# Softmax over rows of 512 on one core: two late tiles of 15 and 13 rows in place of four, and the first load issued by SyncE

## Chip, cores, metric

One core of a Trainium2 chip. The metric is the device time of one execution in microseconds (us), median of several executions. The span is the time from the first to the last instruction of the program in the profile; it is 1.8 us shorter than the device time.

## The reference

The input is 16 x 1024 x 512 in float32, 33.55 MB; so is the output.

```python
def reference(x):                       # x: (16, 1024, 512) float32
    x_scaled = x / 2.0
    x_max = np.max(x_scaled, axis=-1, keepdims=True)
    exp_x = np.exp(x_scaled - x_max)
    return (exp_x / np.sum(exp_x, axis=-1, keepdims=True)).astype(np.float32)
```

## The kernel before

The 16,384 rows are laid over 128 partitions, so each partition has 128 rows of 2 KB; "row" from here on means one such row in all partitions (262,144 B). A buffer of 100 rows in SBUF holds the tiles. PLAN lists them: the chunks of rows that are computed together, and the place in the buffer. The first eight tiles (100 rows) are loaded at once; the tiles t8 to t11 reuse the place of stored ones and must wait for those stores.

```python
PLAN = [
    ([3], 0), ([4, 3], 3), ([5] * 3, 10), ([5] * 3, 25), ([5] * 3, 40), ([5] * 3, 55),
    ([5] * 3, 70), ([5] * 3, 85), ([5] * 3, 10), ([4, 3], 3), ([3], 0), ([3], 25),
]
ARENA = 100
LAG = 2
AFTER = {8: 4, 9: 4, 10: 4, 11: 6}    # late load t8 is issued after the exps of tile 4, ...
FUSED = {1, 2, 3}
...
def issue_loads(begin, end):           # tiles 0 and 1 ahead of the start-up barrier
    for t in range(begin, end):
        if t not in behind:            # behind: tiles that reuse another's place
            nc.scalar.dma_start(out=sb(t), in_=dram(xf, t)).then_inc(ld[t], 16)
...
        # ACT (ScalarE): late loads between the exps; exp with the sum accumulated
        for k, (t, b, c, a) in enumerate(chunks):
            while late and last_chunk[AFTER[late[0]]] < k:
                u = late.pop(0)
                for v in behind[u]:
                    nc.scalar.wait_ge(st[v], 16)
                nc.scalar.dma_start(out=sb(u), in_=dram(xf, u)).then_inc(ld[u], 16)
            ...                        # c exps, the first waits for the chunk's max
        # DVE (VectorE): max of chunk k, then reciprocal and multiply of chunk k - 2
        for k in range(len(chunks) + LAG):
            if k < len(chunks):
                do_max(k)              # waits for the tile's load
            if k >= LAG:
                do_mul(k - LAG)        # waits for the chunk's exps
        # SP (SyncE): a tile is stored when its last chunk is multiplied
        for t in range(len(tiles)):
            nc.sync.wait_ge(s_mul, last_chunk[t] + 1)
            nc.sync.dma_start(out=dram(of, t), in_=sb(t)).then_inc(
                st[t] if t in awaited else s_end, 16
            )
        # GpSimd closes the program
        for t in awaited:
            nc.gpsimd.wait_ge(st[t], 16)
        nc.gpsimd.wait_ge(s_end, 16 * (len(tiles) - len(awaited)))
```

Of the kernel before, what the change touches and what calls it, by code (L numbers as in the profile page):

```python
# [1 line left out]

# [4 lines left out]




PLAN = [
    ([3], 0), ([4, 3], 3), ([5] * 3, 10), ([5] * 3, 25), ([5] * 3, 40), ([5] * 3, 55),
    ([5] * 3, 70), ([5] * 3, 85), ([5] * 3, 10), ([4, 3], 3), ([3], 0), ([3], 25),
]
ARENA = 100
LAG = 2

AFTER = {8: 4, 9: 4, 10: 4, 11: 6}

FUSED = {1, 2, 3}  # L20


@with_exitstack
def kernel(
    ctx: ExitStack,
    tc: tile.TileContext,
    x: bass.AP,
    out: bass.AP,
):
    nc = tc.nc  # L30
    fp32 = mybir.dt.float32

    xf = x.flatten_outer_dims()
    of = out.flatten_outer_dims()
    N, D = xf.shape
    P = nc.NUM_PARTITIONS
    n_rows = N // P
    assert sum(sum(c) for c, _ in PLAN) == n_rows

    arena = nc.alloc_sbuf_tensor("arena", (P, ARENA, D), fp32)  # L40
    negmax = nc.alloc_sbuf_tensor("negmax", (P, n_rows), fp32)
    sums = nc.alloc_sbuf_tensor("sums", (P, n_rows), fp32)
    recip = nc.alloc_sbuf_tensor("recip", (P, n_rows), fp32)



    tiles, chunks, base = [], [], 0
    for t, (cs, at) in enumerate(PLAN):
        r = sum(cs)
        tiles.append((base, r, at))  # L50
        o = 0
        for c in cs:
            chunks.append((t, base + o, c, at + o))
            o += c
        base += r
    last_chunk = {c[0]: k for k, c in enumerate(chunks)}

    def dram(ap, t):
        b, r, _ = tiles[t]
        return ap[b * P : (b + r) * P].rearrange("(p r) d -> p r d", r=r)  # L60

    def sb(t):
        _, r, at = tiles[t]
        return arena[:, at : at + r, :]


    behind = {}
    for t, (_, r, at) in enumerate(tiles):
        for u in range(t):
            _, ru, au = tiles[u]  # L70
            if at < au + ru and au < at + r:
                behind.setdefault(t, []).append(u)

    ld = [tc.alloc_semaphore(f"ld{t}") for t in range(len(tiles))]
    awaited = sorted({u for us in behind.values() for u in us})
    st = {t: tc.alloc_semaphore(f"st{t}") for t in awaited}
    s_end = tc.alloc_semaphore("s_end")
    s_max = tc.alloc_semaphore("s_max")
    s_exp = tc.alloc_semaphore("s_exp")
    s_rec = tc.alloc_semaphore("s_rec")  # L80
    s_mul = tc.alloc_semaphore("s_mul")

    def issue_loads(begin, end):

        for t in range(begin, end):
            if t not in behind:
                nc.scalar.dma_start(out=sb(t), in_=dram(xf, t)).then_inc(ld[t], 16)

    def do_max(k):
        t, b, c, a = chunks[k]  # L90
        nc.vector.reduce_max(  # L91
            out=negmax[:, b : b + c],
            in_=arena[:, a : a + c],
            axis=mybir.AxisListType.X,
            negate=True,
        )._wait_ge(ld[t], 16).then_inc(s_max, 1)

    def do_mul(k):
        t, b, c, a = chunks[k]
        nc.vector.reciprocal(  # L100
            out=recip[:, b : b + c], in_=sums[:, b : b + c]
        )._wait_ge(s_exp, k + 1).then_inc(s_rec, 1)
        if t in FUSED:
            nc.vector.tensor_mul(  # L104
                out=arena[:, a : a + c],
                in0=arena[:, a : a + c],
                in1=recip[:, b : b + c].unsqueeze(2).to_broadcast([P, c, D]),
            )._wait_ge(s_rec, k + 1).then_inc(s_mul, 1)
            return
        for r in range(c):  # L110
            ins = nc.vector.tensor_scalar_mul(  # L111
                out=arena[:, a + r],
                in0=arena[:, a + r],
                scalar1=recip[:, b + r : b + r + 1],
            )
            if r == 0:
                ins._wait_ge(s_rec, k + 1)
        ins.then_inc(s_mul, 1)

    def compute_and_store():  # L120

        late = sorted(behind)
# [6 lines that stand above are left out]
            for r in range(c):  # L129
                ins = nc.scalar.activation(  # L130
                    out=arena[:, a + r],
                    in_=arena[:, a + r],
                    func=mybir.ActivationFunctionType.Exp,
                    bias=negmax[:, b + r : b + r + 1],
                    scale=0.5,
                    accum_out=sums[:, b + r : b + r + 1],
                )
                if r == 0:
                    ins._wait_ge(s_max, k + 1)
            ins.then_inc(s_exp, 1)  # L140


        for k in range(len(chunks) + LAG):
            if k < len(chunks):
                do_max(k)
            if k >= LAG:
                do_mul(k - LAG)
# [5 lines that stand above are left out]
                st[t] if t in awaited else s_end, 16  # L153
            )

        for t in awaited:
            nc.gpsimd.wait_ge(st[t], 16)
        nc.gpsimd.wait_ge(s_end, 16 * (len(tiles) - len(awaited)))



    hook = nc.inst_callbacks[-1]
    nc.remove_inst_callback(hook)
    symbolic = nc._always_lower_symbolic_ap
    nc._always_lower_symbolic_ap = False
    here = str(nc.cur_bb)
    entry = nc.main_func.blocks[0]
    head, jumps = entry.instructions[:-5], entry.instructions[-5:]
    entry.instructions = []
    nc.switch_bb("main", None)  # L170
    issue_loads(0, 2)
    first = list(entry.instructions)
    at = next(k for k, i in enumerate(head) if type(i).__name__ == "InstDrain")
    entry.instructions = head[:at] + first + head[at:]
    issue_loads(2, len(tiles))
    compute_and_store()
    entry.instructions = list(entry.instructions) + jumps
    nc.switch_bb(here, None)
    nc._always_lower_symbolic_ap = symbolic
    nc.push_inst_callback(hook)  # L180


# [1 line left out]
_INS = ['x']  # L184
_OUTS = [((16, 1024, 512), 'float32')]


# [23 lines left out]
```

## Time and profile before

| | before |
|---|---|
| device time | 162.19 us (162.18 to 162.22, 4 runs) |
| span | 160.4 us |
| first DMA packet starts, last one ends | 1.14 us, 158.94 us |
| DVE's last multiply ends | 152.6 us |
| last store issued | 152.62 us |

Three kinds of numbers are used. The page gives busy shares over the span and over 40 equal slices. The table of stretches gives, for each stretch of time, each engine's busy time and what the DMA engines moved in it. The trace also has one record for every DMA packet (start, duration, size, queue); packet times and the ends of the 16 DMA engines are worked out from these records. They do not name the engine, so "the slowest engine" is the last packet to end, and "the mean engine" comes from joining packets end to start into 16 chains. The lines themselves stand in the prediction.

### The profile page before, as it was taken

To read this page: it belongs to the slowest core of one execution; us is meant where nothing else is said; L and a number is where in the kernel's file an instruction comes from. 1 tells how busy PE (TensorE), PEld (TensorE's weight loads), DVE (VectorE), ACT (ScalarE), POOL (GpSimd) and SP (SyncE) were. 2 spreads that over 40 slices of the span, in tenths; PEclk is the share of its full clock that TensorE was granted. 3 is DMA by queue.
4 is the path that set the end of the run, shared out by engine and by line. 5 is a ranking of instruction groups with operands and counts; after the bars stand their busy time and mean duration, and the time that the engine had idled before them with its cause. 6 is when DMAs were issued, how large, how long until landed. Compare 5 with 4: busy or idle time off the path is not lost.

```text
span 160.4 us, 480 instructions
## 1 busy us (share of the span) xinstructions
DVE 132.0 (82%) x155; ACT 94.5 (59%) x257; POOL 0.2 (0%) x4
## 2 busy tenths in 40 slices
DVE  0475499999999999999999999999999997704900
ACT  0739076759548646866679666697666875500500
POOL 0000000000000000000000000000000000000000
DMA  7999999999998999999999999998999999999796
GB/s 259 483 402 467 397 426 411 343 464 420 417 483 383 475 391 467 429 429 439 414 460 406 467 391 469 398 467 376 474 432 423 441 429 432 411 448 432 335 408 245
DMA packets 3459, 67.13 MB, mean 419 GB/s; under 512 B 384, under 2 KB 384, under 8 KB 1152
## 3 DMA queue, kind: packets, MB, share of 16 engines
q10 hardware_dynamic: 1728, 33.56, 49.5%
q1 hardware_dynamic: 1728, 33.56, 48.8%
q14 instruction: 3, 0.02, 0.0%
HBM read 33.55 MB, written 33.55 MB: 418 GB/s over the span
## 4 chain that ended last, share of the span: by engine, by line
DVE 49%; DMA 38%; another core or an unknown queue 5%; ACT 1%; issue 0%; DVEq 0%
DMA arena<-in_x_dram 38%; DVE negmax L91 25%; DVE arena L104 13%; DVE arena L111 10%; ACT arena L130 1%; DVE recip L100 1%; DVEq L206 0%
## 5 line engine op out<-in xcount | busy, mean ns | idle before, releaser
L130 ACT ACTIVATE arena<-arena,negmax 128x512 f32<-128x512 f32 x128 | 90.8, 710 | 51.6 <-DVE negmax L91 51.6
L91 DVE TENSOR_REDUCE negmax<-arena 128x5 f32<-128x2560 f32 (+2 forms) x28 | 72.3, 2586 | 19.6 <-DMA arena<-in_x_dram 19.5
L111 DVE TENSOR_SCALAR arena<-arena,recip 128x512 f32<-128x512 f32 x91 | 37.9, 482 | 0.7
L130 ACT ACTIVATION_READ_ACCUMULATOR arena<-arena,negmax 128x1 f32 x128 | 23.9, 187 | 0.0
L104 DVE TENSOR_TENSOR arena<-arena,recip 128x2560 f32<-128x2560 f32 (+2 forms) x8 | 21.0, 2625 | 0.3
L100 DVE RECIPROCAL recip<-sums 128x5 f32<-128x5 f32 (+2 forms) x28 | 4.9, 176 | 0.0
L130 ACT ACT_TABLE_LOAD x1 | 1.3, 1283 | 4.5 <-issue 4.5
L195 POOL MEMSET const-bfloat16-1.0<- 128x1 bf16 x1 | 0.1, 101 | 0.0
L195 POOL MEMSET const-uint8-127<- 128x1 uint8 x1 | 0.1, 101 | 0.0
L195 POOL MEMSET const-float32-0.0<- 128x1 f32 x1 | 0.1, 98 | 0.2 <-issue 0.2
L195 POOL MEMSET const-float32-1.0<- 128x1 f32 x1 | 0.1, 98 | 0.0
## 6 DMA issues: line engine op xcount, KB each, us to landing
arena<-in_x_dram ACTq DMA_DIRECT2D x7, 3840.0 KB, 44.9
out_dram<-arena SPq DMA_DIRECT2D x7, 3840.0 KB, 23.1
arena<-in_x_dram ACTq DMA_DIRECT2D x2, 1792.0 KB, 33.1
out_dram<-arena SPq DMA_DIRECT2D x2, 1792.0 KB, 11.7
arena<-in_x_dram ACTq DMA_DIRECT2D x3, 768.0 KB, 52.2
out_dram<-arena SPq DMA_DIRECT2D x3, 768.0 KB, 6.7
```

Source lines behind the costliest of these rows:

```text
L91: nc.vector.reduce_max(out=negmax[:, b : b + c], in_=arena[:, a : a + c], axis=mybir.AxisListType.X, negate=True,)._wait_ge(ld[t], 16).the ...
L100: nc.vector.reciprocal(out=recip[:, b : b + c], in_=sums[:, b : b + c])._wait_ge(s_exp, k + 1).then_inc(s_rec, 1)
L104: nc.vector.tensor_mul(out=arena[:, a : a + c], in0=arena[:, a : a + c], in1=recip[:, b : b + c].unsqueeze(2).to_broadcast([P, c, D]),)._w ...
L111: ins = nc.vector.tensor_scalar_mul(out=arena[:, a + r], in0=arena[:, a + r], scalar1=recip[:, b + r : b + r + 1],)
L130: ins = nc.scalar.activation(out=arena[:, a + r], in_=arena[:, a + r], func=mybir.ActivationFunctionType.Exp, bias=negmax[:, b + r : b + r ...
L195: nc = _bacc.Bacc("TRN2", target_bir_lowering=False, num_devices=1)
```

## The change

The four late tiles of 15, 7, 3 and 3 rows become two of 15 and 13 rows, placed at the start of the buffer. The first load goes from ACT to SyncE, so that the first two loads are issued by two engines at the same time. GpSimd's four waits for stores that the late loads already depend on are dropped. The intent is fewer, larger transfers and an earlier start. A line that differs in whitespace alone is cut.

```diff
-    ([5] * 3, 70), ([5] * 3, 85), ([5] * 3, 10), ([4, 3], 3), ([3], 0), ([3], 25),
+    ([5] * 3, 70), ([5] * 3, 85), ([5] * 3, 0), ([5, 4, 4], 15),
 ]
...
-AFTER = {8: 4, 9: 4, 10: 4, 11: 6}
+AFTER = {8: 4, 9: 6}
...
         for t in range(begin, end):
-            if t not in behind:
+            if t in behind:
+                continue
+            if t == 0:
+                nc.sync.dma_start(out=sb(t), in_=dram(xf, t)).then_inc(ld[t], 16)
+            else:
                 nc.scalar.dma_start(out=sb(t), in_=dram(xf, t)).then_inc(ld[t], 16)
...
-        for t in awaited:
-            nc.gpsimd.wait_ge(st[t], 16)
         nc.gpsimd.wait_ge(s_end, 16 * (len(tiles) - len(awaited)))
```

## The prediction

> **What bounds the kernel now.** I read the page first, parts 1 to 3, to see which resource is full for the whole span.
>
> ```profile
> span 160.4 us, 480 instructions
> DVE 132.0 (82%) x155; ACT 94.5 (59%) x257; POOL 0.2 (0%) x4
> DVE  0475499999999999999999999999999997704900
> DMA  7999999999998999999999999998999999999796
> q10 hardware_dynamic: 1728, 33.56, 49.5%
> q1 hardware_dynamic: 1728, 33.56, 48.8%
> ```
>
> The reader is to see two nearly full rows. DVE is solid from slice 6 to slice 32, but has idle slices at both ends. The DMA row has no hole: the load queue (q10) and the store queue (q1) together take 98.3% of what 16 engines can give in the span. So bytes bound this kernel, and DVE is a close second that must only not starve the stores.
>
> Second, the table of stretches (us, DVE busy, ACT busy, POOL busy, clock, DMA share, GB/s) for the end, where this change acts.
>
> ```profile
> 130.00:140.00 10.00, 8.07 (x15) 5.94 (x17) 0.00 (x0) 1.00 0.98 420
> 140.00:145.00 5.00, 0.00 (x0) 0.00 (x0) 0.00 (x0) 1.00 1.06 452
> 145.00:150.00 5.00, 3.28 (x7) 1.57 (x5) 0.00 (x0) 1.00 0.94 406
> 150.00:152.00 2.00, 1.97 (x6) 0.66 (x2) 0.00 (x0) 1.00 0.82 344
> 152.00:154.00 2.00, 0.59 (x2) 0.00 (x0) 0.00 (x0) 1.00 1.01 423
> ```
>
> DVE does nothing from 140 to 145, and still the DMA engines are full. The only weak place is 150 to 152. (A share takes a packet whole at its start, so it can exceed 1; clipping the packet records at the edges of the stretch, I find 0.75 there, 0.98 for 148 to 150 and 1.00 or more in every stretch of 2 us from 2 to 148.) The bubble is 2 x 0.25 + 2 x 0.02 = 0.54 us of mean engine time, all there is to win by better feeding.
>
> Third, the timeline of DVE, for why the last loads are late.
>
> ```profile
> 126.24 2.28 DVE L91 TENSOR_REDUCE negmax<-arena 128x4 f32<-128x2048 f32 x1
> 135.70 1.75 DVE L91 TENSOR_REDUCE negmax<-arena 128x3 f32<-128x1536 f32 x1 [1.11 <-DMA arena<-in_x_dram]
> 146.65 1.75 DVE L91 TENSOR_REDUCE negmax<-arena 128x3 f32<-128x1536 f32 x1 [7.40 <-DMA arena<-in_x_dram]
> 151.32 1.28 DVE L111 TENSOR_SCALAR arena<-arena,recip 128x512 f32<-128x512 f32 x3
> ```
>
> The last load, 768 KB, lands at 146.6, 11.0 us after the one before it, although 0.79 MB alone would take under 2 us. The traffic of the stretch 126 to 142 shows why (packets, MB, share of 16 engines):
>
> ```profile
> q1 hardware_dynamic: 218, 5.71, 82.8%
> q10 hardware_dynamic: 220, 1.25, 18.7%
> ```
>
> Equal packets, very unequal bytes: each DMA engine takes one load packet, then one store packet. A packet here is one partition's rows. The trace's DMA records give its time: 234 ns for 6,144 B (3 rows), 535 ns for 14,336 B (7 rows), 1,138 ns for 30,720 B (15 rows). A tile puts 8 packets on each engine, so 3 rows against a 15-row store need 8 x (234 + 1138) = 11.0 us, as seen.
>
> **What the Trainium skill says.** The page "DMA: Bandwidth & Descriptors", section "Queues, rings and completion order", says that an engine goes round-robin over the queues with work, a packet at a time. The trace agrees (218 against 220 packets). Its section "Issuing engines are not separate DMA queues" says that issuing from several engines saves only the sequencer's issue time; this trace has ACT at 376 ns for the first issue, and no run here yet shows SyncE issuing a load. Its section "Where 436 GB/s comes from" has a ceiling of 435.2 GB/s for the 16 ports. Taking that figure, 67.11 MB need an estimated 154.2 us; the first packet starts at 1.14 us and the last ends at 158.93, so 157.8 us are used, and only some 3.6 us could go even with perfect packets. The page "Perfetto Trace Analysis", section "What “DMA-bound” means", counts engines that are full as a bound and says larger descriptors are what matters then; the change does go that way, but from packets that are already 6 KB and more.
>
> **The change part by part.** The tiles t0 to t8 keep their sizes, 3, 7 and seven of 15 rows. The last 13 rows were three tiles (7, 3, 3) and become one (13, in chunks of 5, 4, 4).
>
> (a) Packets. Per queue and engine the three tiles took 8 x (535 + 234 + 234) = 8.02 us. A 13-row packet has 26,624 B; between the 7- and 15-row packets the time grows by 603 ns per 16,384 B, so I estimate 1138 - 0.151 x 1000 = 987 ns, and 8 x 987 = 7.90 us. Saved: 0.13 us per queue, 0.25 us for both; four semaphore writes of 9 ns less make 0.29 us. This lies on the bounding resource and counts in full.
>
> (b) The order of loads and stores. The 13-row load gets almost half the engine against 15-row stores: 8 x (987 + 1138) = 17.0 us. The load before it ends at 109.92 in the records, so its packets end at 126.9 and, with the 1.5 us from last packet to landing that t8 and t11 show, it lands near 128.4 instead of having its last part at 146.6. That only moves bytes: stores done in that time are fewer by as much.
>
> (c) Does DVE still feed the stores? A step of 5 rows takes 2.73 (max) + 0.1 + 2.07 (multiply) = 4.93 us. Maxes of t8 start at 111.45, 116.4, 121.3; the multiply of t8's first chunk ends at 126.3. DVE then waits to 128.4 for the 13 rows, does max of 5 (to 131.2), multiply (133.4), max of 4 at 2.28 (135.6), multiply (137.8): t8's store goes out near 137.8, against 134.6 before. Then max of 4 (139.9), multiply 5 (142.1), multiplies of 4 at 1.8 (143.9, 145.7): the last store goes out near 145.8, against 152.6. The store queue meanwhile: t7's store, pushed back by the larger load packets, ends near 141.0 to 141.6; t8's 9.1 us end at 150.1 to 150.7; the last 7.9 us end near 158.4. Each store is queued 3 us or more before its turn, so the bubble at 150 to 152 goes.
>
> (d) What that bubble is worth. Little: before, the engines end t8's store between 149.83 and 150.80, and the next store's packets start at 150.65 to 150.80. The fast engines waited, the slowest hardly did. Landing needs all 16, so I credit 0.08 us of the 0.54.
>
> (e) The first load on SyncE. SyncE's first instruction stands at 0.00, ACT's first issue at 0.13, so the first packet may come 0.13 us earlier. The 0.4 us of ACT's second issue are no gain: t1's packets start at 3.25, when t0's are through. The cost: t0 and t1 now alternate, t0 ends after 8 x (234 + 535) = 6.2 us and lands near 8 instead of 4.6. DVE's work on t0 and t1 (1.75 + 3.94 + 0.2 + 1.28 = 7.2 us) then ends near 15.2, before t2 lands at 18.05; hidden.
>
> (f) Four waits less on GpSimd at the end: their stores landed by about 85 us (62.0 + 23.1), long done; zero.
>
> Sum: 0.29 + 0.08 + 0.13 = 0.50 us; 162.19 - 0.50 = 161.7 us.
>
> **The rivals.** First, the tail becomes exposed: a last store of 3.4 MB instead of 0.8 MB, after a last load of 13 rows. If compute came late, up to 13 rows of compute and a whole store would stand alone, 5 to 8 us more (167 to 170). For it speaks the size; against it, that load lands 18 us sooner and the store queue has 9.1 us of t8 to move after 141. If t8's store alone were late by 1 us past its turn, it would cost 1 us (162.7). Second, the bubble counts in full for all engines and the barrier, with ACT issuing one load less before it, comes 0.4 us sooner: then 0.29 + 0.54 + 0.4 = 1.2 us, 161.0. Against it: the slow engine, and the queue being full by then. Third, the late landing of t0 holds up DVE, which has no slack between 18 and 109: for each us that t2's first max is late, t8's max is late too. There is about 3 us of slack before 18.05, so this gives nothing, and even 1 us of it would be hidden behind the queued stores. Fourth, all is hidden, and SyncE's issue is no earlier: 161.9.
>
> **Range and chances.** The sure term is 0.29; the others are 0 to 0.9 together, with a small chance of a starved store. I predict 161.7 us, and 161.1 to 162.2 eight times in ten. Faster by 2% would need below 158.9, more than the estimated slack of the bytes leaves together with start and landing: 0.01. Slower by 2%, above 165.4, needs the exposed tail: 0.03. Within 2%: 0.96.
>
> **What would show it right or wrong.** (a) 1,440 packets per queue instead of 1,728, and 13-row packets near 987 ns. (b) The last load landing at 127 to 130 and DVE's longest late wait falling from 7.4 to about 2 us. (c) Stores issued near 138 and 146, and no weak stretch at 150 to 152. (d) Time after the last issue grows from 7.7 us to 14 or so without harm. (e) First max near 8, max of t2 still near 18. Wrong if DMA share falls below 0.9 anywhere from 128 to 158, if t2's max moves past 19, or if 13-row packets are slower than 1,000 ns.

## The result, and the profile after

The changed kernel takes 161.61 us (161.53 to 161.81, 4 runs), against 162.19 us. The ratio is 0.9966, with a 95% interval of 0.9948 to 0.9983. A ratio here is the mean time of one kernel's fast runs over the mean of the other's in the same rounds, so it is not quite the ratio of the medians. Executions over 1.5% slower than the fastest of the same kernel are left out of the means. The profiled run was the slowest of the four, 161.81 us.

The page of the changed kernel:

```profile
span 160.0 us, 474 instructions
DVE  0294599999999999999999999999999499993000
DMA  7999999999999999999999999999999999999993
q1 hardware_dynamic: 1584, 34.34, 50.1%
q10 hardware_dynamic: 1296, 32.77, 48.1%
```

The reader sees that DVE now ends nearly two slices (7.1 us) earlier and that the DMA row is all nines to the last slice. The packets, 2,880 in both queues, were 3,456 before. They are split 1,584 to 1,296 and not 1,440 each, because the first load's 144 packets now run in SyncE's queue; I had forgotten that in the list of what would show.

The table of stretches for the end:

```profile
140.00:145.00 5.00, 4.93 (x14) 2.66 (x8) 0.00 (x0) 1.00 0.97 418
145.00:150.00 5.00, 0.48 (x2) 0.00 (x0) 0.00 (x0) 1.00 1.06 457
150.00:152.00 2.00, 0.00 (x0) 0.00 (x0) 0.00 (x0) 1.00 0.99 426
152.00:154.00 2.00, 0.00 (x0) 0.00 (x0) 0.00 (x0) 1.00 0.99 426
```

The weak stretch from 150 to 152 is gone (426 GB/s where there were 344), and DVE works from 140 to 145, where it had waited for the last load.

The timeline of DVE:

```profile
7.01 5.61 DVE L96 TENSOR_REDUCE negmax<-arena 128x3 f32<-128x1536 f32 x3 [7.01 <-DMA arena<-in_x_dram]
17.73 2.82 DVE L96 TENSOR_REDUCE negmax<-arena 128x5 f32<-128x2560 f32 x1 [3.72 <-DMA arena<-in_x_dram]
...
128.08 2.82 DVE L96 TENSOR_REDUCE negmax<-arena 128x5 f32<-128x2560 f32 x1 [2.08 <-DMA arena<-in_x_dram]
...
143.81 1.67 DVE L116 TENSOR_SCALAR arena<-arena,recip 128x512 f32<-128x512 f32 x4
```

The first max starts at 7.01 (4.69 before), that of the third tile at 17.73 (18.08 before). The last load makes DVE wait 2.08 us at 128.08, in place of 7.40 us at 146.65. The last multiply ends at 145.5 and not at 152.6. The last store then takes 13.5 us to land where it took 6.7, because the store queue still has the 15-row tile to move.

So compute ends 7.1 us earlier and the program 0.4 to 0.6 us earlier. The first is no gain by itself; the experiments ask where the second comes from.

### The profile page after: what moved, and what is told of

It reads as the page before. It is cut to its first block, busy times and chain, and to the rows that moved or that the text cites. A ratio compares the mean times of both kernels' runs of the same rounds, so it can differ in the third digit from the quotient of the medians.

```text
span 160.0 us, 474 instructions
## 1 busy us (share of the span) xinstructions
DVE 131.6 (82%) x153; ACT 94.4 (59%) x257; POOL 0.2 (0%) x4
## 3 DMA queue, kind: packets, MB, share of 16 engines
q1 hardware_dynamic: 1584, 34.34, 50.1%
q10 hardware_dynamic: 1296, 32.77, 48.1%
## 4 chain that ended last, share of the span: by engine, by line
DVE 58%; DMA 32%; issue 0%; DVEq 0%; ACT 0%
DMA arena<-in_x_dram 32%; DVE negmax L96 30%; DVE arena L116 13%; DVE arena L109 13%; DVE recip L105 1%; DVEq L209 0%; ACT arena L135 0%
## 6 DMA issues: line engine op xcount, KB each, us to landing
out_dram<-arena SPq DMA_DIRECT2D x1, 3328.0 KB, 13.5
```

## The experiments

Twelve kernels ran in four groups. Each group shares one chip and its runs of the kernel before, whose medians were 162.14, 162.18, 162.21 and 162.16 us; single runs of it ranged from 161.91 to 162.77, wider than in the first comparison. All results were correct.

### The changed kernel again

> The changed kernel once more, as the yardstick of this group. 161.6 us again, ratio near 0.9966, if the first four runs (161.53 to 161.81) were typical. The profile should again show a spread of about 1 us between the first and the last DMA engine to run dry at the end.

Measured: 161.53 us (161.29 to 162.09, 6 runs), ratio 0.9962 (0.9945 to 0.9980). In the packet records the mean engine ends at 157.77 and the slowest at 158.50. The gain holds. Note how it is made up: before, the mean engine ended at 158.84 and the slowest at 158.94. So the mean engine gained 1.1 us and the slowest only 0.4 (0.2 in the first profile, where it ends at 158.73), and the program waits for the slowest.

### The first load alone

```diff
             if t == 0:
+                nc.sync.dma_start(out=sb(t), in_=dram(xf, t)).then_inc(ld[t], 16)
+            else:
                 nc.scalar.dma_start(...)
```

> The kernel before, with only the first load moved to SyncE. My step (e) credits 0.13 us (SyncE's first instruction stands 0.13 us before ACT's first issue): 162.06 us, ratio 0.9992. Rival: the start counts with the whole 0.5 us by which the barrier comes sooner in the changed kernel (0.84 against 1.34 us): 161.7, ratio 0.997. Rival: it gives nothing, since both engines' first packets wait for the same thing: 162.19. In each case the first max moves from 4.7 to about 7 us and the max of the third tile stays near 17.7 to 18.1.

Measured: 161.84 us, ratio 0.9977 (0.9962 to 0.9992), so 0.13 to 0.62 us. My 0.13 is at the edge; the size in the middle is 0.37. The table of stretches for the first microsecond of transfers, first in the kernel before, then in this one:

```profile
1.00:2.00 1.00, 0.00 (x0) 0.00 (x0) 0.00 (x0) 1.00 0.85 197
```

```profile
1.00:2.00 1.00, 0.00 (x0) 0.00 (x0) 0.00 (x0) 1.00 0.92 276
```

The first packet starts 0.14 us sooner (1.00 against 1.14), and between 1 and 2 us the transfers run at 276 GB/s and not at 197. I first read this as a quicker filling of the DMA engines, but it does not show that: the stretch begins at 1.00 in both, so the earlier start alone adds an estimated 59 GB/s (0.14 us at 420 GB/s). Counted in the packet records from each kernel's own first packet, the first microsecond moved 183 to 242 KB in nine kernels with the first load on SyncE and 193 to 230 KB in four with it on ACT. The third tile's max starts at 17.74; over the first profiles it started at 17.73 to 17.77 with SyncE and at 17.95 to 18.08 without. That is 0.26 us on average, twice my term; where the rest of it comes from is not shown.

### The tiles alone

```diff
-            if t == 0:
+            if t < 0:                  # so ACT issues every load
                 nc.sync.dma_start(...)
```

> The changed kernel, with the first load back on ACT: the two late tiles (and the missing waits) alone. My sum gives 0.29 for packets and 0.08 for the bubble: 161.82 us, ratio 0.9977. If the bubble counts in full: 0.29 + 0.54, 161.36, ratio 0.995. If the tiles give nothing and the start all: 162.19.

Measured: 161.67 us, ratio 0.9968 (0.9953 to 0.9984): 0.52 us in the middle, with 0.37 expected. The two parts measured alone add to 0.89 us, against 0.62 us for both in the same group; each has about 0.25 us of uncertainty, so they may add without interaction. What is shown is that both parts contribute. This run does not separate the packets from the new order of loads and stores, the closed hole and the missing waits; the next ones take up the hole and the waits.

### The bubble alone

```diff
+            if k == len(chunks) - 1:
+                do_mul(k - 2)
+                do_mul(k - 1)
             if k < len(chunks):
                 do_max(k)
-            if k >= LAG:
+            if k >= LAG and k - LAG not in (len(chunks) - 3, len(chunks) - 2):
                 do_mul(k - LAG)
```

> The kernel before with the same DMAs, but the multiplies of the two chunks ahead of the last one are put before the last max, which waits for the last load. So the stores of the 7-row tile and of the first late 3-row tile go out near 140.6 and 142.0 instead of 149.8 and 151.2, and the bubble of 0.54 us of mean engine time at 148 to 152 closes, with the packets unchanged. My step (d): the slowest engine never waited there, so at most 0.1 us is gained: 162.1, ratio 0.9995; and the engines no longer end together (spread 0.17 us before) but about 1 us apart. Rival: the bubble counts in full: 161.65, ratio 0.9967.

Measured: 162.20 us, ratio 1.0003 (0.9985 to 1.0022). The table of stretches shows that the hole really closed (388 GB/s where the kernel before had 344, with shares clipped at the edges 1.00):

```profile
150.00:152.00 2.00, 1.15 (x4) 0.78 (x3) 0.00 (x0) 1.00 0.91 388
```

The two stores went out at 140.8 and 142.2 instead of 149.8 and 151.2, and nothing was gained; the rival's 0.9967 is outside the interval, while my 0.08 us cannot be told from zero. In the records of the profiled run, the slowest of the six (162.81 us), the engines end between 157.65 and 159.62 us, the mean one at 158.14; before, all ended between 158.77 and 158.94. The hole was time in which the fast engines waited for the slowest, and the last store lands only when that one is done.

### GpSimd's waits put back

```diff
+        for t in awaited:
+            nc.gpsimd.wait_ge(st[t], 16)
         nc.gpsimd.wait_ge(s_end, 16 * (len(tiles) - len(awaited)))
```

> The changed kernel with the four waits of GpSimd put back. My step (f) says they cost nothing, as those stores landed by about 85 us: 161.6 us, ratio 0.9964, and 0.80 us from the last packet's end to SyncE's next instruction, as in the two profiles of the changed kernel. Rival: the 0.90 us in the three profiles with the old tail are the waits' doing: 161.7, and 0.90 us again here.

Measured: 161.68 us, ratio 0.9959 (0.9941 to 0.9977); the time cannot tell 0.1 us. The trace can: from the end of the last packet to SyncE's next instruction it is 0.89 us here, as in the kernels with the waits (0.89 to 0.90), against 0.80 to 0.84 without them. The opposite edit settles it.

### The kernel before, without the waits

```diff
-        for t in awaited:
-            nc.gpsimd.wait_ge(st[t], 16)
         nc.gpsimd.wait_ge(s_end, 16 * (len(tiles) - len(awaited)))
```

> The kernel before without GpSimd's four waits, one look. From the end of the last packet to SyncE's next instruction the profiles with the waits show 0.89 to 0.90 us (four kernels) and those without 0.80 to 0.84 (six). If the waits are the cause: 0.80 to 0.84 here, with the old tail of three small stores. If it is the tail of small stores: 0.90.

One look, its state unknown: 162.49 us, and 0.81 us from the last packet's end, with the old small stores. So in the profiles the four waits cost 0.09 us at the end of the program, although the stores they wait for had landed 70 us before. The instruction records show how, which I had overlooked. In the four kernels with the waits, GpSimd's wait for the last stores stands in an instruction of its own (EVENT_SEMAPHORE, at 159.308 us in the kernel before), and the closing branch starts 0.086 to 0.087 us after it. In the ten without them that instruction is missing, and the branch itself carries the wait. The cost is one more instruction after the last landing.

### A larger dose of packets

```diff
+            if t == len(tiles) - 1:
+                for j in range(13):    # one store per row
+                    nc.sync.dma_start(out=dram(of, t)[:, j : j + 1, :],
+                                      in_=arena[:, at + j : at + j + 1, :]).then_inc(s_end, 16)
+                continue
```

The lines that set `at` and raise the count that GpSimd waits for are cut.

> The changed kernel, its last store cut into 13 stores of one row, all issued after the last multiply (145.5 us; the 13 issues of about 0.34 us end at 150, and the first has 4 us until its turn). It is a larger dose of the packet term of step (a). By the line between the measured packets a packet of 2,048 B takes about 83 ns: 8 x (13 x 83 - 987) = 0.74 us, and 12 more semaphore writes of 9 ns per engine 0.11 us: 162.45 us, ratio 1.0015. If only bytes counted: 161.6, ratio 0.9965. If short pieces are slower in memory than the line says: above 163.

Measured: 161.97 us, ratio 0.9981 (0.9962 to 0.9999): 0.2 to 0.4 us more than the changed kernel (by the ratios and by the medians), at most half of what I expected. The intervals of the two ratios overlap, so the time alone does not show it; the records do. A 2,048 B packet is recorded with 84 ns, as the line said. But the stores follow each other every 0.645 us on an engine, 80.6 ns for each of 8 packets with the semaphore write included, so the records overlap by a little. 13 x 0.645 = 8.39 us against 7.90 for one store of 13 rows is 0.49 us, or 5 ns for each of the 96 packets more. So packets do cost beyond their bytes, but at this size about half of what the line between recorded durations gives.

### A real hole in the feed

```diff
-            nc.sync.wait_ge(s_mul, last_chunk[t] + 1)
+            nc.sync.wait_ge(s_mul, last_chunk[min(t + (t == len(tiles) - 2), len(tiles) - 1)] + 1)
```

> The changed kernel, with the store of the 15-row tile held back until the last multiply is done: it goes out near 145.5 instead of 137.5 us, while the store queue runs empty at 140.4 to 141.6. It tests step (c) and the first rival, an exposed tail: a hole in the feed that the slowest engine does see has to count in full. First packet near 145.5 + 0.83 = 146.3, so the slowest engine waits 4.7 us: 161.6 + 4.7 = 166.3 us, ratio 1.025, with all engines ending within 0.3 us of each other. Rival: the DMA engines make some of it up (they were slowed by something that a pause cures): under 165.5.

Measured: 166.43 us (165.70 to 166.82), ratio 1.0250 (1.0222 to 1.0277), as expected to 0.1 us.

```profile
140.00:142.00 2.00, 1.96 (x7) 2.00 (x6) 0.00 (x0) 1.00 0.15 61
142.00:144.00 2.00, 1.97 (x7) 0.19 (x2) 0.00 (x0) 1.00 0.00 0
144.00:146.00 2.00, 1.02 (x3) 0.00 (x0) 0.00 (x0) 1.00 0.51 215
```

The DMA share is zero from 142 to 144 while DVE works. The held store is issued at 145.05 and its first packet starts at 145.88, the 0.83 us that I had taken from the kernel before. All engines end within 0.16 us of each other. So a hole that the slowest engine sees is paid in full, and step (c) was right that the change lives from its 3 us of margin there.

### Fewer, larger tiles in the middle

```diff
-    ([3], 0), ([4, 3], 3), ([5] * 3, 10), ([5] * 3, 25), ([5] * 3, 40), ([5] * 3, 55),
-    ([5] * 3, 70), ([5] * 3, 85), ([5] * 3, 0), ([5, 4, 4], 15),
+    ([3], 0), ([4, 3], 3), ([5] * 3, 10), ([5] * 5, 25), ([5] * 5, 50),
+    ([5] * 5, 75), ([5] * 3, 0), ([5, 4, 4], 15),
```

AFTER and FUSED were restated by chunk, so that the late loads and the multiplies keep nearly the same places.

> A try at a better version by the same term: the changed kernel with the five middle tiles of 15 rows (75 rows) made three of 25 rows, the chunks for compute, and so the programs of DVE and ACT, left as they are. Two tiles less: by the line a 51,200 B packet takes 1,892 ns, so 3 x 8 x 1892 against 5 x 8 x 1138 saves 0.11 us per queue, plus two semaphore writes: 0.26 us for both queues. 161.35 us, ratio 0.9948. Rival: the larger stores come too late and the store queue runs dry after the loads are through: above 162, with a weak stretch between 115 and 125 us. Rival: 50 KB packets don't follow the line: 161.6 or more.

Measured: 163.45 us, ratio 1.0085 (1.0054 to 1.0116). A miss. The list of waits:

```profile
DVE negmax L96 <- DMA arena<-in_x_dram: 12.3, 4, 6.5
ACT arena L135 <- DMA out_dram<-arena: 10.4, 1, 10.4
ACT L135 <- issue: 3.2, 1, 3.2
DVE recip L105 <- ACT arena L135: 3.0, 1, 3.0
```

The second line is new: ACT stood 10.4 us before a late load, waiting for the store of the tile whose place it takes. Packets of 30 KB in the store queue against 50 KB in the load queue had slowed that store, and it landed at 79.7 us where the changed kernel had it at 66.7. The packets themselves follow the line (1,891 ns, 1,892 expected). The load queue ran dry from 78.0 to 84.2 us; the DMA engines stayed full with stores, yet packets between 80 and 100 us were slower than their usual time by 0.85 us per engine in sum. The changed kernel has 0.02 there. That is not all: from 40 to 60 us, before the load queue ran dry, the same sum is 0.67 us (0.07 in the changed kernel), and after 100 us 0.38 (0.04). Over the whole run it is 2.8 us against 1.35, and this agrees with the mean engine's end (159.21 against 157.76). So the time went into slow packets, about half of them around the restart of the load queue; why they are slow stays open.

The mended form keeps the first 40 rows as they were:

```diff
-    ([3], 0), ([4, 3], 3), ([5] * 3, 10), ([5] * 3, 25), ([5] * 3, 40), ([5] * 3, 55),
-    ([5] * 3, 70), ([5] * 3, 85), ([5] * 3, 0), ([5, 4, 4], 15),
+    ([3], 0), ([4, 3], 3), ([5] * 3, 10), ([5] * 3, 25), ([5] * 4, 40),
+    ([5] * 4, 60), ([5] * 4, 80), ([5] * 3, 0), ([5, 4, 4], 15),
```

> The mended form of the eight-tile kernel, which had failed because ACT waited 10.4 us for a store before it could issue a late load, and the load queue ran dry meanwhile. Here the first 40 rows keep their tiles, so the late loads wait for the same stores as in the changed kernel, and only the last 60 of the middle rows go in three tiles of 20 instead of four of 15. One tile less: by the line between the measured packets 4 x 8 x 1138 - 3 x 8 x 1515 ns, 0.06 us per queue, with the semaphore writes 0.14 us for both: 161.45 us, ratio 0.9955, which the noise may well hide. If ACT is blocked again or the load queue runs dry: above 162.

Measured: 162.17 us, ratio 1.0004 (0.9991 to 1.0018). A miss again. ACT waited 2.4 us for a store. In the records the mean engine ends at 157.80, as in the changed kernel (157.77), but two engines end at 159.06 and 159.20. Why these two are late stays open. No version that beats the changed kernel came out of this.

### The first two loads on SyncE

```diff
-            if t == 0:
+            if t < 2:
                 nc.sync.dma_start(...)
```

> The changed kernel with the first two loads both issued by SyncE, one after the other. It splits the gain of the start: with the first load on SyncE the third tile's max began at 17.73, 17.77 and 17.74 us, with it on ACT at 18.08, 17.95 and 17.99, so 0.26 us sooner, twice my 0.13. If only SyncE's earlier start counts: first packet near 1.0, third tile's max still near 17.75, and about 161.6 us. If two engines issuing at once fill the DMA engines sooner (246 to 276 GB/s against 197 to 203 from 1 to 2 us): back to about 200 GB/s there, third tile's max near 17.88, and about 161.7 us. The first max comes back to about 4.5 us in both cases.

Measured: 161.68, 161.83, 163.47 and 163.64 us in the four fast runs, ratio 1.0015 (0.9972 to 1.0058); two more, 164.68 and 165.95, are slow, and the median of all six is 163.56. No other kernel spreads so far, and the reason stays open. It could not split the start, because I had overlooked the alternation of packets that I had used elsewhere:

```profile
4.43 1.75 DVE L96 TENSOR_REDUCE negmax<-arena 128x3 f32<-128x1536 f32 x1 [4.43 <-DMA arena<-in_x_dram]
16.66 3.95 DVE L96 TENSOR_REDUCE negmax<-arena 128x4 f32<-128x2048 f32 x2 [10.48 <-DMA arena<-in_x_dram]
```

The 7-row load in SyncE's queue alternates with the 15-row load in ACT's, 14 KB against 30 KB, and lands at 16.7 us instead of 8.6. DVE is then 4.2 us late with the third tile (21.92). From 1 to 2 us the rate was 240 GB/s, between the two groups of numbers; its first packet starts at 1.03 us, and as said above this stretch cannot tell a quicker filling from an earlier start. So what the changed kernel gains at the start beyond SyncE's 0.13 us stays open.

### More instruction fetches

```diff
+        for j in range(512):
+            nc.gpsimd.memset(scratch[0:1, j : j + 1], 0.0)
         nc.gpsimd.wait_ge(s_end, 16 * (len(tiles) - len(awaited)))
```

The line that allocates `scratch` is cut.

> What spreads the DMA engines at the end? In the profiles of the changed kernel the mean engine ends at 157.8 us and the slowest at 158.5 to 158.7. Three instruction fetches of 8 KB lie in each span (near 30, 75 and 100 us, 0.31 us each) and the packet after each is slower by 0.1 to 0.35 us; on one engine they would be some 1.1 us, about the whole spread, but the records do not name the engine. Here GpSimd, idle otherwise, writes 512 single elements, so more instructions have to be fetched; nothing waits for them. At 64 B an instruction (three fetches of 128 for some 400 instructions of ACT and DVE) four more fetches. If all fetches fall on one engine and set the end: the slowest engine ends 4 x (0.31 + 0.1 to 0.35) = 1.6 to 2.6 us later, 163.2 to 164.2 us in all, the mean engine only 0.1 to 0.2 later. If each falls on another engine: under 0.7 us more, 161.6 to 162.3. If fetches have nothing to do with it: 161.6, and the same spread. More than the fetches could be slow: if GpSimd's writes slow DVE, its last multiply ends later than 145.5, which costs nothing up to about 3 us.

Measured: 163.26 us (162.68 to 163.61), ratio 1.0058 (1.0043 to 1.0073). The queue of instruction fetches in the page, first of the changed kernel, then of this one with the new work:

```profile
q14 instruction: 3, 0.02, 0.0%
```

```profile
q14 instruction: 7, 0.06, 0.1%
...
L163 POOL MEMSET scratch<- 1x1 f32 x512 | 17.1, 88 | 4.5 <-issue 4.0
```

Four fetches more, 32 KB beside 67 MB. One DMA engine ends at 160.53 us, the next at 158.25, the mean one at 157.95. DVE's last multiply ends at 146.6 us, 1.1 us later than in the changed kernel, because the last load lands that much later; its last store goes out 2.9 us ahead of its first packet. So something of the new work loads one engine, and that engine sets the end: 1.65 us for four fetches. Each takes 0.31 us itself, and packets behind some of them are slower by 0.1 to 0.35 us.

I had concluded that the three fetches of the changed kernel fall on this engine too and make its spread (0.73 and 0.97 us between the mean and the slowest engine in two profiles). The packet records refute that. Joined with the order of each queue kept, they leave little choice after 40 us: in the first profile of the changed kernel every packet then starts 3 or 4 ns before the end of the one before it. There the fetches at 75 and at 100 us lie on two engines that both end at 158.19, and the slowest, 158.73, carries neither; in the second profile they lie on engines that end at 158.32 and 158.10, and the slowest ends at 158.50. In this run the three old fetches lie on engines that end at 158.25 and 158.23, and three of the four new ones on the engine that ends at 160.53 (the fourth comes too early to be placed). That engine also has four packets between 40 and 105 us that are slow by 0.19 to 0.42 us with no fetch beside them, so not all of its delay is the fetches' own. What makes the slowest engine of the changed kernel slow stays open.

## Why the prediction was right, point by point

The time (161.7 predicted, 161.61 measured) and the class were right. Its steps:

- (a) Packets, 0.29 us: the 13-row packet was recorded with 987 ns, as worked out. The tiles alone gave 0.52 us in the middle of their interval, with the waits and whatever the bubble is worth in it; less 0.09 for the waits this leaves 0.43 (0.17 to 0.67), which 0.29 fits, but no run isolates the packets. The dose of one-row stores cost about half of the expectation in the records, so the term exists and its size for much smaller packets is overstated; for the sizes of the change the records do not overlap (the 3-row stores follow each other every 1.88 us, 8 x 234 ns + 9 ns).
- (b) and (c) The order of transfers and the feed: right to less than half a microsecond (max at 128.08 for 128.4, stores issued at 137.53 and 145.51 for 137.8 and 145.8). The late store showed what the margin is worth. Two additions in (c) are wrong: 2.73 + 0.1 + 2.07 is 4.90 and not 4.93, and 137.8 + 2.28 is 140.1 and not 139.9, which would put the last store near 146.0.
- (d) The bubble, 0.08 us: right in kind, and its own experiment gave nothing (1.0003). The program waits for the slowest engine, as I had it; why that engine is slow is not known, and those of the three instruction fetches that could be placed are not on it. One sign that I had set for being wrong came true here: with shares clipped at the edges, the DMA share is 0.84 from 156 to 158, because the engines no longer end together.
- (e) The first load on SyncE, 0.13 us: mis-sized. The first packet came 0.13 us sooner, as worked out, but the third tile's max came 0.26 us sooner, and what the other half comes from is not shown. The load t0 landed near 7 and not 8, because t1's packets started only at 2.27 us; the two loads do not start together, as I had assumed.
- (f) The waits, 0: wrong by 0.09 us, shown in both directions in the profiles. That the stores had long landed was right; that the wait for the last stores moves into an instruction of its own was overlooked.

With 0.29 for (a) as worked out, and the rest as measured at different places in the profiles, the sum is 0.29 + 0 + 0.26 + 0.09 = 0.64 us, against 0.58 us by the medians. Three terms were off, by +0.13, +0.09 and -0.08 us, and partly cancelled; with intervals of about 0.3 us to either side, that the time came within 0.1 us is partly luck. The first rival, the exposed tail, was put to the test and needs a late store to appear; the second asked for the full bubble, which is refuted; the third, a delay of DVE by the late first load, did not happen (17.73, and not later); the fourth, that SyncE's issue is no earlier, is refuted by the first packet (1.00 against 1.14 us).

## What to carry to other kernels

Where two DMA queues are both full, think in packets: they alternate one for one, so a small load beside large stores crawls, and making the late loads as large as the stores brings them forward, even though the total hardly changes. A hole in the mean DMA share is worth only what the slowest of the 16 engines sees of it: ask first when that one is done, and whether closing the hole lets the others merely end sooner. On a kernel that is full of bytes from start to end, what was left here is tenths of a microsecond in the packets, the start and the closing waits. More instructions are not free either: 512 on an idle engine cost 1.65 us.

## What the Trainium skill lacked or had wrong

- "DMA: Bandwidth & Descriptors", section "Queues, rings and completion order": the round-robin by packet agrees with the traces, but what follows for bytes is not said. A load of 0.79 MB in packets of 6,144 B beside stores in packets of 30,720 B took 11.0 us.
- The same page, section "Bandwidth", rates a single 1 MB transfer, a load issued by GpSimd, at 78% of the peak. It does not say what holds behind a full queue, and there the figure is no guide: the 0.79 MB stores of the kernel before follow each other every 1.88 us, an estimated 418 GB/s, 96% of the page's 435.2.
- The same page, section "Issuing engines are not separate DMA queues", says that issuing from several engines saves only issue time. It leaves out that this also changes the order of the packets: at the start t0 landed at 7.0 in place of 4.7 us, and with two loads on SyncE the second landed at 16.7 in place of 8.6.
- No page that I know of says which of the 16 DMA engines carry the instruction fetches of 8 KB: at least three of four that GpSimd's 512 instructions added lie on one engine, which ended 2.3 us after the next one.
- No page that I know of says what a wait costs that needs an instruction of its own: 0.086 to 0.087 us until the next one starts, at the end of GpSimd's program.
